# A constant product first, memory ahead of weights, deeper gate buffers, half of K later, two output products exchanged

## The chip, the cores and the metric

The kernel runs on one core of a Trainium2 chip. A core has a matrix engine (TensorE, PE in the profile; its weight loads are PEld), a vector engine (VectorE, DVE), a scalar engine (ScalarE, ACT), GpSimd (POOL) and SyncE (SP), each with an instruction line of its own that it works off in order, and 16 DMA engines that all queues share. SP, ACT and POOL issue the DMAs here. The metric is the device time of one execution in microseconds, lower is better; each time is the median of several runs.

## The reference

One block of a hybrid encoder on 512 frames of width 1024, all in float32:

```python
h = rms_norm(x, norm_mix_g)
proj = h @ w_in + b_in                       # 1024 -> 4864 columns
y_a = rwkv7_branch(proj[..., :1792], ...) @ w_branch_a
y_b = rglru_branch(proj[..., 1792:2304], proj[..., 2304:2816], ...) @ w_branch_b
merged = sigmoid(proj[..., 2816:3840]) * y_a + sigmoid(proj[..., 3840:]) * y_b
x = x + merged @ w_mix_out
x = x + cross_attention(rms_norm(x, norm_x_g), rms_norm(mem, norm_mem_g), w_cq, w_ckv, w_co)
x = x + conv_ffn(rms_norm(x, norm_ffn_g), w_ffn_in, ffn_conv_w, ffn_conv_b, w_ffn_out)
return rms_norm(x, norm_final_g)
```

Cross-attention has 4 heads of 256 channels over a memory of 256 rows; K and V are the two halves of `rms_norm(mem) @ w_ckv`. The conv FFN has 2816 hidden channels, a causal convolution of width 3 on the gate, and a GELU.

## The kernel before

Everything is kept with channels on the 128 partitions and the 512 frames along the free dimension; a "block" is 128 channels. A dense product is a sum over blocks of 128 input channels. For accuracy each operand is split into a high part in PE's fast float32 type and a low rest, and each 128 x 128 unit of weights gives three PE products (`mm3`, lines 161 to 163: high by high, high by low, low by high). Weights are streamed from DRAM in pieces of 512 KB, eight units each, through four raw buffers (`stream`, lines 96 to 117; `Units`, lines 132 to 149): SP issues the load, ACT casts the high part (line 115), DVE subtracts to get the low part (line 116); there are three buffers each for high and low.

The program text is not the order on the engines. A planner with a model of each instruction's duration sorts the instructions by a priority (the order of the text; `tc.high_priority` puts a block ahead) into a fixed line for each engine, before the kernel runs. `tc.keep_in_program_order`, `tc.issue_after` and `tc.add_manual_dep` fix the place of single instructions. A tile with `bufs=n` has n buffers in turn; a write into a buffer waits until the last reader of the tile n places before is done, and an instruction that waits holds up everything behind it in its engine's line.

The stages, in order:

- **Start (lines 269 to 303).** The memory (1 MB, tile `mraw`, four pieces of 256 KB, `load_m`) and the parameters `pv` are loaded. For K the memory is scaled with its norm's gain and split (lines 286 to 290, tile `m2`), its squares are summed (lines 291 to 294, `mss`) and turned into `rm`, the scale of each row of memory. SP's first loads are: memory piece 0, half of w_k's first piece, memory 1, the other half, memory 2, w_k's second piece, memory 3.
- **K and V (lines 306 to 348).** Eight blocks of K, 24 PE products of 256 columns each, written to DRAM through `kt`; then V, while x is loaded and normalised (`x_norm`, lines 323 to 330).
- **Small parameters (lines 354 to 397).** Constants of the two branches are worked out on DVE in the tile `dp`, from `pv`.
- **Projection and branches (lines 521 to 935).** 38 blocks of w_in (`inproj`), with the recurrences between them. The 16 gate blocks go to DRAM (`dG`). `NSUM` (line 517) says how many of POOL's DRAM-to-DRAM sums of FFN weights are released by each block (`sum_behind`): they prepare a Strassen-like scheme with seven products instead of eight for both FFN matrices.
- **Merge (lines 945 to 968).** For each of 8 blocks, w_branch_b's product (12 PE products of 512 columns) is multiplied with its gate `gb`, loaded back from `dG` by SP into two buffers (line 947); then the same for w_branch_a with `ga` (line 961, two buffers), whose result is added and split into `mg2`. The mix product (line 992) reads all of `mg2`.
- **Attention (lines 1018 to 1079).** K and V are loaded back by ACT's queue in four pieces (K's first half, V, V, K's second half) through two buffers `kv`, and split. Then for each head the scores, a softmax (`ex`, line 1057), the product with V, and in between the next head's q.
- **FFN in (lines 1141 to 1243)** and **FFN out (lines 1253 to 1374)**. FFN out is seven products over 4 x 11 units each, 132 PE products of 256 columns, named A11, A12, s1, s2, s3, s4, A22, in this order, with operands in three sets. `X` and `YZ` are their sums in PSUM. A product's weights named s come from DRAM (`dO`), where POOL has summed them; those of s4 are summed on top of those of s2 once these have been read (line 1366). Where a partial result is needed twice it is copied (`p1`, `p5`, `p6`). `ffn_out` adds a block to the residual `xr`, squares it and scales it with the final gain; `final` normalises a range of frames and stores it. The first half of the frames ends with A22 (`c21`, in two pieces of 128 frames, the last thing that is done), the second with s4 (`c12`).

Of the kernel before, what the change touches and what calls it, by code (L numbers as in the profile page):

```python
# [17 lines left out]
P = 128  # L18
T = 512
# [14 lines left out]
NMID = 10  # L34
IN_ORDER = IN_RWKV + IN_REST
# [19 lines left out]
def hybrid_block_kernel(ctx: ExitStack, tc: tile.TileContext, xT_d, mT_d, pv_d, cst_d, win_d, wk_d, wv_d,  # L55
# [213 lines left out]
    with tc.tile_pool(name="p0", bufs=1, reuse_waits="tile") as p0:  # L269
        ln_exp_set()  # L270
# [15 lines left out]
        for k in range(KB):  # L286
            g = par("nmem", k)
            S.activation(m2[:, 0, k, :], mraw[:, k, :], AF.Identity, scale=g)
            V.scalar_tensor_tensor(m2[:, 1, k, :], mraw[:, k, :], g, m2[:, 0, k, :].bitcast(F32),
                                   ALU.mult, ALU.subtract)  # L290
# [15 lines left out]
        for m in range(KB):  # L306
# [5 lines left out]
            kt = p0.tile([P, NMEM], F32, tag="kt", name=f"kt{m}", bufs=4)  # L312
            V.tensor_tensor(kt, ps[:, :NMEM], rm, ALU.mult)
# [40 lines left out]
        dp = cp.tile([P, 80], F32, name="dp")  # L354
        omu = dp[:, 0:14]
        V.tensor_scalar(omu, parall("mu"), -1.0, 1.0, ALU.mult, ALU.add)
        qb = dp[:, 14:28]
        V.tensor_tensor(qb, pv[:, PV["b_in"][0]:PV["b_in"][0] + 14], omu, ALU.mult)
        oka = dp[:, 28:32]
        V.tensor_scalar(oka, parall("k_a"), -1.0, 1.0, ALU.mult, ALU.add)  # L360

        cw = parall("cbw")
        bx = par("b_in", 14, 4)
        cbias = dp[:, 32:36]
        ccor = dp[:, 36:48].rearrange("p (j b) -> p j b", b=4)
# [1086 lines left out]
```

## Time and profile before

| | us |
|---|---|
| median of 3 runs | 908.43 (905.87 to 909.82) |
| the profiled execution, own time | 911.28 |
| its span | 909.5 |
| PE busy | 886.1 |
| DVE busy | 684.8 |
| ACT busy | 515.8 |

The span runs from the first instruction that the profiler saw to the last; 1.8 us of the execution's own time lie around it. "Busy" counts the time in which an engine has an instruction under way. In rows of the timeline the columns are start, duration, engine, line, operation, output <- inputs, shape, count, and in brackets the idle time before it with what ended it. PE's products overlap: a row lasts longer than the distance to the next one, and it is this distance that counts.

### The profile page before, as it was taken

Reading aid. Unit: us, or ns where it says so; the run is one execution under the profiler, and the core shown is the slowest. Engines: PE = TensorE matmul, PEld = TensorE weight load, DVE = VectorE, ACT = ScalarE, POOL = GpSimd, SP = SyncE. Lnnn points to the kernel's source line nnn. Section 1 sums busy time; section 2 is a strip of 40 time slices with the busy share of each in tenths; the row PEclk is TensorE's granted clock in tenths of the full one; section 3 lists DMA queues with packets and bytes.
Section 4 is the critical chain, followed back from the end, with each engine's and each line's share of the span. In section 5 each row is a group of like instructions: output and inputs, shape, how many; then the busy total and the mean of one; then the engine's idle time right before and its main releaser. Section 6 shows DMA issues by size and latency. Waiting matters only on the chain.

```text
span 909.5 us, 15907 instructions
## 1 busy us (share of the span) xinstructions
PE 886.1 (97%) x6186; PEld 769.3 (85%) x6186; DVE 684.8 (75%) x1100; ACT 515.8 (57%) x787; POOL 131.2 (14%) x161
## 2 busy tenths in 40 slices
PE   6999999999999999989989999999999999999996
PEld 6888878888877777768867778999999999999996
DVE  7884698768957686576566568889888888999674
ACT  6674676643347675134454356766655556757563
POOL 0102222021001122001012111111111111202100
PEclk9999999999999999999999999999999999999999
DMA  8879799677876289968887958899989998988963
GB/s 273 279 269 222 191 234 226 201 200 215 264 175 161 41 176 239 261 189 229 220 215 164 214 124 184 243 273 275 271 240 301 268 284 252 245 274 207 273 193 92
DMA packets 97642, 201.37 MB, mean 221 GB/s; under 512 B 19424, under 2 KB 30816, under 8 KB 97504
## 3 DMA queue, kind: packets, MB, share of 16 engines
q1 hardware_dynamic: 63584, 118.97, 40.0%
q0 software_dynamic: 25504, 67.38, 36.4%
q10 hardware_dynamic: 8480, 14.02, 4.5%
q8 instruction: 48, 0.79, 0.3%
q14 instruction: 26, 0.21, 0.1%
HBM read 188.54 MB, written 78.12 MB: 293 GB/s over the span
## 4 chain that ended last, share of the span: by engine, by line
PE 86%; DMA 7%; DVE 5%; ACT 1%; issue 1%; SPq 0%; DVEq 0%; ACTq 0%
PE in_ps L162 8%; PE in_ps L161 8%; PE in_ps L163 7%; PE fx_ps L162 5%; PE fx_ps L161 5%; PE fx_ps L163 5%; PE fyz_ps L162 3%; PE fyz_ps L163 3%; PE fyz_ps L161 3%; DMA gb<-dG 2%; PE ox_ps L163 2%; PE ox_ps L161 2%; PE ox_ps L162 2%; PE co_ps L161 2%; PE co_ps L163 2%; PE co_ps L162 2%
## 5 line engine op out<-in xcount | busy, mean ns | idle before, releaser
L127 ACT CAST wfi_h<-wfi_r 128x1024 fp32r<-128x1024 f32 x77 | 81.0, 1052 | 81.0 <-PE fyz_ps L162 28.4
L162 PE MATMUL in_ps<-hT,win_h 128*128 128x512 f32 x304 | 121.6, 402 | 0.0
L161 PE MATMUL in_ps<-hT,win_h 128*128 128x512 f32 x304 | 121.5, 401 | 0.1
L163 PE MATMUL in_ps<-hT,win_l 128*128 128x512 f32 x304 | 121.6, 401 | 0.0
L128 DVE TENSOR_TENSOR wfi_l<-wfi_r,wfi_h 128x1024 fp32r<-128x1024 f32 x77 | 94.1, 1222 | 23.0 <-ACT wfi_h L127 22.9
L427 POOL DMA_DIRECT2D dS<-in_wfi x66 | 66.5, 1028 | 267.8 <-PE in_ps L161 134.1
L116 DVE TENSOR_TENSOR win_l<-win_r,win_h 128x1024 fp32r<-128x1024 f32 x38 | 46.3, 1222 | 30.8 <-ACT win_h L115 30.1
L161 PEld LDWEIGHTS in_ps<-hT,win_h 128*128 128x128 f32 x304 | 57.0, 188 | 14.6 <-DVE pr L531 0.6
L162 PEld LDWEIGHTS in_ps<-hT,win_h 128*128 128x128 f32 x304 | 57.0, 188 | 14.5 <-issue 0.7
L163 PEld LDWEIGHTS in_ps<-hT,win_l 128*128 128x128 f32 x304 | 57.0, 188 | 14.2 <-issue 0.7
L463 POOL DMA_DIRECT2D dOs<-in_wfo x54 | 39.9, 789 | 188.4 <-PE fyz_ps L161 48.2
L115 ACT CAST win_h<-win_r 128x1024 fp32r<-128x1024 f32 x38 | 39.8, 1048 | 43.1 <-PE in_ps L162 40.4
L1279 DVE TENSOR_TENSOR wfo_l<-wfo_r,wfo_h 128x1024 fp32r<-128x1024 f32 (+1 forms) x39 | 47.1, 1209 | 16.2 <-ACT wfo_h L1278 14.6
L1278 ACT CAST wfo_h<-wfo_r 128x1024 fp32r<-128x1024 f32 (+1 forms) x39 | 40.4, 1038 | 30.2 <-DMA wfo_r<-dOs 8.0
L163 PE MATMUL ox_ps<-go,wfo_l 128*128 128x256 f32 x176 | 49.5, 281 | 1.2 <-DVE wfo_l L1279 1.2
L162 PE MATMUL fx_ps<-hr,wfi_h 128*128 128x256 f32 x176 | 49.8, 283 | 0.0
L161 PE MATMUL ox_ps<-go,wfo_h 128*128 128x256 f32 x176 | 49.8, 283 | 0.0
L163 PE MATMUL fx_ps<-hr,wfi_l 128*128 128x256 f32 x176 | 49.8, 283 | 0.0
L162 PE MATMUL fx_ps<-hq,wfi_h 128*128 128x256 f32 x176 | 49.4, 281 | 0.0
L162 PE MATMUL fyz_ps<-hq,wfi_h 128*128 128x256 f32 x176 | 49.4, 281 | 0.0
L161 PE MATMUL fx_ps<-hr,wfi_h 128*128 128x256 f32 x176 | 49.4, 280 | 0.0
L162 PE MATMUL ox_ps<-go,wfo_h 128*128 128x256 f32 x176 | 49.3, 280 | 0.0
(419 smaller groups left out, 2713.4 us busy)
## 6 DMA issues: line engine op xcount, KB each, us to landing
dS<-in_wfi POOLq DMA_DIRECT2D x66, 512.0 KB, 7.9
wfi_r<-dS SPq DMA_DIRECT2D x44, 512.0 KB, 6.3
win_r<-in_win SPq DMA_DIRECT2D x38, 512.0 KB, 5.6
wfi_r<-in_wfi SPq DMA_DIRECT2D x33, 512.0 KB, 5.9
dS<-dS POOLq DMA_DIRECT2D x22, 512.0 KB, 5.3
dOs<-in_wfo POOLq DMA_DIRECT2D x12, 512.0 KB, 7.1
wv_r<-in_wv SPq DMA_DIRECT2D x8, 512.0 KB, 4.9
dG<-gs ACTq DMA_DIRECT2D x16, 256.0 KB, 5.2
```

Source lines behind the costliest of these rows:

```text
L115: S.copy(hi[:, o:o + n], raw[:, o:o + n])
L116: V.tensor_tensor(lo[:, o:o + n], raw[:, o:o + n], hi[:, o:o + n].bitcast(F32), ALU.subtract)
L127: S.copy(hi, raw)
L128: V.tensor_tensor(lo, raw, hi.bitcast(F32), ALU.subtract)
L161: first = PE.matmul(ps, lh, rh, start=start, stop=False, **kw)
L162: PE.matmul(ps, lh, rl, start=False, stop=False, **kw)
L163: PE.matmul(ps, ll, rh, start=False, stop=stop, **kw)
L427: return lambda: nc.gpsimd.dma_start(s(out), src, **kw)
L463: yield lambda k=k, w=w, src=src: nc.gpsimd.dma_start(dO[n, m][:, k * P:(k + w) * P], src, **kw)
L1278: S.copy(hi[:, :n], raw[:, :n])
L1279: V.tensor_tensor(lo[:, :n], raw[:, :n], hi[:, :n].bitcast(F32), ALU.subtract)
```

## The change

The functions stay; the edits are these.

- **Start.** Ten PE products of a constant come first. The memory's gain is loaded by itself (`gm`, 8 columns) ahead of `pv`, which is issued later. SP's order becomes memory 0, half of w_k's piece, memory 1, the other half, memory 2, memory 3, w_k's second piece. The split of the memory is given high priority, the squares come after the last split, and `kt` has six buffers.
- **Small parameters.** The block is unchanged and comes behind the last evacuation of K.
- **NSUM.** Block 37 releases one sum, 17, 18 and 19 one more each, 20 two and 21 three fewer.
- **Merge.** `gb` takes turns over three tags with two buffers each, `ga` has five buffers.
- **Attention.** Three `kv` buffers; K's second half is loaded in the text after the first head.
- **FFN out.** A22 before s4. The copies `p6` go; the sum after s2 is added to `xr` at once. `c21` normalises the first half of the frames in one piece, `c12` the second in two pieces of 128.

```diff
+NWAKE = 10
+KVB = 3
...
-    wdma = []
+    wdma, mdma = [], []
...
                     elif len(wdma) == 1:
-                        tc.add_manual_dep(ins.ins, wdma[0].ins.name, mybir.DependencyInfo(
+                        tc.add_manual_dep(ins.ins, mdma[-1].ins.name, mybir.DependencyInfo(
...
+        wake = rw_ps("wake")
+        with tc.high_priority():
+            for i in range(NWAKE):
+                PE.matmul(wake, onesr, onesr.unsqueeze(1).to_broadcast([P, 4, P]), start=True, stop=True)
+        gm = cp.tile([P, KB], F32, name="gm")
+        o = PV["nmem"][0]
+        tc.keep_in_program_order(nc.scalar.dma_start(gm, pv_d[:, o:o + KB]))
         ln_exp_set()
...
-                tc.keep_in_program_order(
-                    nc.sync.dma_start(mraw[:, 2 * q:2 * q + 2, :], mT_d[:, 2 * q:2 * q + 2, :]))
-
-        nc.scalar.dma_start(pv, pv_d)
+                mdma.append(tc.keep_in_program_order(
+                    nc.sync.dma_start(mraw[:, 2 * q:2 * q + 2, :], mT_d[:, 2 * q:2 * q + 2, :])))
+
         load_m(0)
+        m2 = p0.tile([P, 2, KB, NMEM], F32R, name="m2")
+
+        def split_m(k):
+            g = gm[:, k:k + 1]
+            hi = S.activation(m2[:, 0, k, :], mraw[:, k, :], AF.Identity, scale=g)
+            V.scalar_tensor_tensor(m2[:, 1, k, :], mraw[:, k, :], g, m2[:, 0, k, :].bitcast(F32),
+                                   ALU.mult, ALU.subtract)
+            return hi
+
+        with tc.high_priority():
+            for k in range(2):
+                split_m(k)
         un = Units(wk_d, "wk")
         un.fill(lambda i: [load_m(q) for q in ((1,), (2, 3))[i]])
-        m2 = p0.tile([P, 2, KB, NMEM], F32R, name="m2")
+        tc.keep_in_program_order(nc.scalar.dma_start(pv, pv_d))
...
-        for k in range(KB):
-            g = par("nmem", k)
-            S.activation(m2[:, 0, k, :], mraw[:, k, :], AF.Identity, scale=g)
...
-        S.activation(mss, mraw[:, 0, :], AF.Square)
+        with tc.high_priority():
+            for k in range(2, KB):
+                last_m = split_m(k)
+        with tc.issue_after(last_m.ins):
+            S.activation(mss, mraw[:, 0, :], AF.Square)
         for k in range(1, KB):
-            S.activation(msq[k], mraw[:, k, :], AF.Square)
+            with tc.issue_after(last_m.ins):
+                S.activation(msq[k], mraw[:, k, :], AF.Square)
...
-            kt = p0.tile([P, NMEM], F32, tag="kt", name=f"kt{m}", bufs=4)
-            V.tensor_tensor(kt, ps[:, :NMEM], rm, ALU.mult)
+            kt = p0.tile([P, NMEM], F32, tag="kt", name=f"kt{m}", bufs=6)
+            last_k = V.tensor_tensor(kt, ps[:, :NMEM], rm, ALU.mult)
...
-        dp = cp.tile([P, 80], F32, name="dp")
+        with tc.issue_after(last_k.ins):
+            dp = cp.tile([P, 80], F32, name="dp")
...
-            17: 3, 18: 4, 19: 4, 20: 4, 21: 4}
+            37: 1, 17: 4, 18: 5, 19: 5, 20: 2, 21: 1}
...
-        gb = tp.tile([P, T], F32, tag="st", name=f"gb{m}", bufs=2)
+        gb = tp.tile([P, T], F32, tag=("ga", "gx", "st")[m % 3], name=f"gb{m}", bufs=2)
...
-        ga = pm.tile([P, T], F32, tag="ga", name=f"gta{m}")
+        ga = pm.tile([P, T], F32, tag="ga", name=f"gta{m}", bufs=5)
...
-    for i, what in ((0, "K"), (0, "V"), (1, "V"), (1, "K")):
-        kv = pk.tile([P, D], F32, tag="kv", name=f"kv{what}{i}", bufs=2)
+
+    def load_kv(what, i):
+        kv = pk.tile([P, D], F32, tag="kv", name=f"kv{what}{i}", bufs=KVB)
...
+    load_kv("K", 0)
+    for i in range(2):
+        load_kv("V", i)
...
         if hd < 3:
             q2 = q_head(hd + 1)
+        if hd == 0:
+            load_kv("K", 1)
...
-        for n in ("A11", "A12", "s1", "s2", "s3", "s4", "A22"):
+        for n in ("A11", "A12", "s1", "s2", "s3", "A22", "s4"):
...
+    def c21(m):
+        sq = ffn_out(X[m], None, ALU.subtract, MQ + m, cols[0], last=m == MQ - 1)
+        if m == MQ - 1:
+            final(cols[0], sq, 2, "x")
+
     def c12(m):
-        sq = ffn_out(YZ[m][:, H:T], p6[m], ALU.add, m, cols[1], last=m == MQ - 1)
-        if m == MQ - 1:
-            final(cols[1], sq, 2)
...
         if m < MQ - 1:
-            ffn_out(X[m], None, ALU.subtract, MQ + m, cols[0])
+            ffn_out(YZ[m][:, H:T], None, ALU.add, m, cols[1])
         else:
-            for o in (0, P):
+            for o in (H, H + P):
                 ts = slice(o, o + P)
-                final(ts, ffn_out(X[m][:, ts], None, ALU.subtract, MQ + m, ts, last=True), 4)
+                final(ts, ffn_out(YZ[m][:, ts], None, ALU.add, m, ts, last=True), 4, "yz")
...
-    out_product("s2", 0, X, False, lambda m: S.copy(p6[m], X[m]))
+    out_product("s2", 0, X, False,
+                lambda m: V.tensor_tensor(xr[:, m, cols[1]], xr[:, m, cols[1]], X[m], ALU.add))
...
+    out_product("A22", 0, X, False, c21)
     out_product("s4", 1, [t[:, H:T] for t in YZ], False, c12)
-    out_product("A22", 0, X, False, c21)
```

More of the change, by code (lines that the diff above doesn't have):

```diff
@@ L351, in hybrid_block_kernel @@
             nc.sync.dma_start(cst, cst_d)
-        dp = cp.tile([P, 80], F32, name="dp")
[L355 to L365, printed above, removed]
@@ L1308, in hybrid_block_kernel @@
     sn1, sn5 = ([pc.tile([P, T], F32, tag="sn", name=f"{n}_{i}", bufs=3) for i in range(2)] for n in ("o1", "o5"))
-    sn6 = pc.tile([P, T], F32, tag="sn", name="o6_0", bufs=3)
     p1, p5 = ([t[:, c] for t in ts for c in cols] for ts in (sn1, sn5))
-    p6 = [sn6[:, c] for c in cols]
-    p6 += [pc.tile([P, H], F32, tag="p5", name=f"o6_{m}", bufs=3) for m in (2, 3)]
     def ffn_out(src, snap, sign, m, ts, first=False, last=False):
@@ L1327, in ffn_out, with final @@
         return sq
-    def final(ts, sq, nb):
+    def final(ts, sq, nb, tag):
         n = ts.stop - ts.start
-        pss = rw_ps(f"rs_ps{ts.start}", pf, "yz", bufs=4)
+        pss = rw_ps(f"rs_ps{ts.start}", pf, tag, bufs=4)
         PE.matmul(pss[:, :n], ones, sso[:, ts], start=True, stop=False)
```

75 lines of the change are left out of this document (41 added, 34 removed).

## The prediction

> **What bounds the kernel now.** I read the page first, then the view of waits for PE (TensorE), because the page says that this engine is the bound.
>
> ```profile
> span 909.5 us, 15907 instructions
> PE 886.1 (97%) x6186; PEld 769.3 (85%) x6186; DVE 684.8 (75%) x1100; ACT 515.8 (57%) x787; POOL 131.2 (14%) x161
> ```
>
> PE is idle for 909.5 - 886.1 = 23.4 us. Nothing in the change removes a needed product, so it can only win from these idle times and from products that run slowly. The view of waits (wait, total us, times, longest) says where they are:
>
> ```profile
> PE k_ps L161 <- ACT m L288: 6.5, 1, 6.5
> PE sc_ps L1050 <- ACT ex L1057: 2.6, 1, 2.6
> PE mix_ps L161 <- ACT mg L967: 1.3, 1, 1.3
> PE ya_ps L161 <- DVE mB L951: 1.3, 2, 0.7
> PE ox_ps L163 <- DVE wfo_l L1279: 1.2, 2, 0.8
> PE mix_ps L162 <- DVE mg L968: 0.7, 1, 0.7
> PE ya_ps L161 <- DVE gta L965: 0.3, 1, 0.3
> ```
>
> Four places: the start (6.5), the merge of the gated branches (ya and mix, 3.6 in five waits), attention (2.6) and the output weights (1.2). They sum to 13.9 us; the other 9.5 I put down to the tail after the last product, which no edit shortens. Each edit aims at one of the four, so I price them in turn, always as later or earlier starts of PE's products.
>
> **1. The start.** The timeline of the first 16 us, and one stretch of the windows (us, then busy time and count for PE, PEld, DVE, ACT, POOL, then clock, DMA share, GB/s):
>
> ```profile
> 1.05 0.23 DVE L198 CAST onesr<-ones 128x128 fp32r<-128x128 f32 x1
> 5.41 0.62 ACT L115 CAST wk_h<-wk_r 128x512 fp32r<-128x512 f32 x1 [0.48 <-DMA wk_r<-in_wk]
> 6.49 0.58 PE L161 MATMUL k_ps<-m,wk_h 128*128 128x256 f32 x1 [6.49 <-ACT m L288]
> 8.22 0.41 PE L163 MATMUL k_ps<-m,wk_l 128*128 128x256 f32 x1
> 8.43 0.41 PE L161 MATMUL k_ps<-m,wk_h 128*128 128x256 f32 x1
> 9.06 0.91 ACT L288 ACTIVATE m<-mraw,pv 128x256 fp32r<-128x256 f32 x2 [0.91 <-DMA mraw<-in_mT]
> 11.55 1.23 DVE L116 TENSOR_TENSOR wk_l<-wk_r,wk_h 128x1024 fp32r<-128x1024 f32 x1
> 12.83 0.39 PE L163 MATMUL k_ps<-m,wk_l 128*128 128x256 f32 x1 [0.47 <-DVE wk_l L116]
> 15.16 0.28 PE L162 MATMUL k_ps<-m,wk_h 128*128 128x256 f32 x1
> 15.27 0.28 PE L163 MATMUL k_ps<-m,wk_l 128*128 128x256 f32 x1
> 6.50:13.00 6.50, 5.91 (x22) 4.89 (x23) 5.83 (x17) 5.59 (x14) 0.00 (x0) 1.00 0.94 361
> ```
>
> At 8 us products start 0.21 us apart, at 15 us 0.115 apart: PE starts at half rate, although the clock column says 1.00. Until 13.0 it does 22 products, which at full rate would be 22 x 0.115 = 2.5 us of work. The ten wake products need only onesr (ready at 1.28). A product of 512 columns at half rate takes about 2 x 0.21 = 0.42 us, so they run from 1.3 to 5.5, before anything real can begin; they cost nothing on PE and no other engine waits for them.
>
> But data sets this stretch as well. The first product can move from 6.49 to the end of the first w_k cast, 5.41 + 0.62 = 6.03, since the first casts of m, for which PE now waits, come ahead of the squares and need the small gm instead of the whole pv. Then four blocks of m give 12 products; the next need the third piece of memory, which landed at 9.06, and its casts (0.45 on ACT, as long on DVE): not before 9.9. With this landing the earliest time for 22 products is 9.9 + 10 x 0.115 = 11.1, a gain of 13.0 - 11.1 = 1.9, and 2.5 if the memory, now whole ahead of w_k's second piece, lands 0.6 sooner. The second piece however lands later, behind 256 KB more, and its casts come after the four of m: ACT is at 9.06 + 4 x 0.45 = 10.9 free for it, and 1.03 and 1.23 us later (the row at 11.55) its low half is there: 13.1. By then PE has done the first piece's 24 products and perhaps 3 more, 5 more than before: 5 x 0.115 = 0.6. I take **-0.8**, near this end because it is the chain that the static order gives, with bounds of -2.5 and +1.5 (the squares later, so that PE's sum over mss stands in its line before mss is ready).
>
> A rule of the Trainium skill (TensorE: Matmul & The Clock Gate, Part 1) bears on the ten products: the gate opens after a busy window of about 3.4 us that runs free of the kernel, so a start may meet it anywhere in its window. By that rule the wake's 4.2 us may or may not hold a whole busy window, and the gate opens between 4.7 and 8.1, an estimate from that page. The trace's 6.49 to somewhere past 8.43 fits it. It changes little here, because the products up to 9.9 wait for data in either case.
>
> The block of small parameters (lines 354 to 397) moves behind the last K evacuation:
>
> ```profile
> L389 DVE TENSOR_TENSOR dp<-dp x7: 155/159/164, 18.2 to 40.9; 128x4 f32<-128x4 f32 x7
> ...
> 36.00:57.00 21.00, 20.98 (x91) 16.50 (x90) 18.55 (x31) 16.77 (x22) 1.08 (x2) 1.00 0.89 302
> ...
> 49.41 1.42 DVE L328 SCALAR_TENSOR_TENSOR hf<-xraw,pv,rx 128x512 f32<-128x512 f32 x2 [0.45 <-ACT rx L214]
> ```
>
> It is 37 DVE instructions of about 0.16 us, 5.9 us (the first row gives the duration and the stretch of seven of them). Until now they filled gaps from the start on; after, they come in the stretch 36 to 57 or later, where DVE is idle 21.00 - 18.55 = 2.45 us and some of them run already. From 49.4 its line is full with the normalised x, for which the first product of w_in waits. What doesn't fit has lower priority than x's chain and can slip behind it, since the scans need only its first two results. I count 0, with +6 as the far end (all of it ahead of x). The deeper kt buffers count 0: no PE wait names kt.
>
> **2. The merge.** DVE waits in the stretch 340 to 410, the DMA view of 345 to 410, and four rows of the timeline:
>
> ```profile
> DVE mB L951 <- DMA gb<-dG: 9.8, 6, 3.0
> DVE gta L965 <- DMA gta<-dG: 3.0, 5, 1.0
> ...
> gb<-dG SPq DMA_DIRECT2D x8, 256.0 KB, 6.7
> gta<-dG SPq DMA_DIRECT2D x8, 256.0 KB, 3.3
> ...
> 344.93 0.50 SPq L948 DMA_DIRECT2D gb<-dG  x1
> 350.52 9.52 SPq L948 DMA_DIRECT2D gb<-dG  x3
> ...
> 373.73 0.40 PE L163 MATMUL yb_ps<-yb,wbb_l 128*128 128x512 f32 x1
> 374.81 0.47 PE L161 MATMUL ya_ps<-ya,wba_h 128*128 128x512 f32 x1 [0.68 <-DVE mB L951]
> ```
>
> With two buffers a gate's load is issued only when the product two blocks back is evacuated, and lands 6.7 us later, while a block lasts 12 x 0.233 = 2.8 us. So the gates are always late, banks of PSUM stay full and PE waits. The last two rows show how a wait is sized: starts are 1.08 apart instead of 0.23, so 0.85 is lost where the view says 0.68. Five waits therefore cost 3.6 + 5 x 0.17 = 4.4 us.
>
> After: gb has six buffers. The yb blocks ended every 2.8 us up to 374.0, the first at 354.4; the seventh load needs the first's buffer, is issued at about 355, lands at 362 and is wanted at 371. All eight are early. gta has five: the sixth needs the first block's buffer, free about 8 us after ya begins, and lands 3.3 to 6.7 later, at 11 to 15; it is wanted at 6 x 2.8 = 17. The eighth's margin is about the same, and the mix reaches the last mg only 21 x 0.233 = 4.9 us after ya's end, against a chain of four 0.7 us steps. So 4.4 could all go. The loads share SP's queue in order with w_ba's and w_mix's pieces, and a load that waits for its buffer holds those up; I leave 0.6 for that: **-3.8**, bounds -4.5 and 0. NSUM takes five POOL sums from the two blocks before the merge and gives four of them to earlier ones; 0, as no PE wait names them.
>
> **3. Attention.** Rows from the timelines of ACT, DVE and PE:
>
> ```profile
> 456.24 1.23 DVE L1029 TENSOR_TENSOR K<-kvK,K 128x1024 fp32r<-128x1024 f32 x1 [1.30 <-ACT K L1028]
> ...
> 458.81 0.38 ACTq L1024 DMA_DIRECT2D kvK<-dK  x1
> ...
> 466.42 1.05 ACT L1028 CAST K<-kvK 128x1024 fp32r<-128x1024 f32 x1 [3.90 <-DMA kvK<-dK]
> ...
> 468.00 0.39 PE L161 MATMUL q_ps<-hx,wq_h 128*128 128x512 f32 x1
> 470.30 0.56 ACT L1057 ACTIVATE ex<-sc_ps,smst,rxc 128x256 f32<-128x256 f32 x1 [1.40 <-DVE smst L1055]
> 471.01 0.39 PE L1050 MATMUL sc_ps<-K,q 128*128 128x256 f32 x1 [2.62 <-ACT ex L1057]
> ```
>
> K's second half is loaded at 458.81, lands 7.6 us later, and ACT stands 3.90 us before its cast, with the first softmax queued behind. PE's starts are 471.01 - 468.00 = 3.01 apart: 2.8 lost. Heads 0 and 1 don't need this half. After, K0, V0, V1 have their own buffers and load at once, and K1's cast comes after the first head. I take **-2.4**, since the first softmax still shares DVE with w_q's low halves. The end on the other side: K1's cast stands in ACT's line elsewhere.
>
> **4. The output.** A row of the chain, and two of the timeline:
>
> ```profile
> 832.75 11.11 DMA wfo_r<-dOs
> ...
> 828.24 1.64 POOL L463 DMA_DIRECT2D dOs<-in_wfo  x2 [25.68 <-DMA wfo_r<-dOs]
> 843.95 2.20 ACT L1278 CAST wfo_h<-wfo_r 128x1024 fp32r<-128x1024 f32 x2 [4.45 <-DMA wfo_r<-dOs]
> ```
>
> The two waits there (1.2 + 2 x 0.17 = 1.5) are for weights of s2 and s3 that load while POOL's sums for s4 run. Those sums are released by s2's loads as before, so swapping s4 and A22 behind s3 leaves both waits. Four ACT copies become four DVE adds and four later adds go: hidden behind PE. The tail after the last product has the same steps with the halves of the columns exchanged. **0**, bounds -1.5 and +1.0.
>
> **Sum.** -0.8 - 3.8 - 2.4 + 0 = -7.0. The profiled execution has a span of 909.5 and took 911.28 by its own time, so it would be 904.3; it is 2.85 above the median of the runs, 908.43, and there the same step gives **901.4 us**.
>
> **Rivals.**
> - The start gains nothing: squares or parameter block meet PE or x's chain. For it: DVE has no gap from 49.4 on. Against: the planner gives both a lower priority. Term 1 becomes +1.5: 903.7.
> - The merge keeps its waits: SP's queue holds a gate behind a weight or a weight behind a gate. For: one queue, 9.52 us for three issues. Against: the margins above. Term 2 becomes -0.6: 904.6.
> - The change doesn't do what it says in attention: K0's buffer falls free at 457.5, so K1 is loaded nearly when it is now and the planner puts its cast in the same place. Term 3 becomes -0.4: 903.4.
> - Slower: K1's cast stands in ACT's line in front of the second head's softmax, before its load has landed. Of the present stand of 3.90 PE lost 2.8, so 1.1 is covered. The longest landing on the chain of waits is 11.1 us; standing for all of it costs 10.0, against the 2.4 won, so term 3 becomes +7.6: 911.4. The kernel is slower than before from a stand of 1.1 + 7.0 = 8.1 us on. For it: ACT's line is fixed in advance and its present stand shows a landing later than planned. Against: after the second head's products there is more than a head's time until K1 is wanted.
> - PE falls back to half rate between 5.5 and 9.9, where it has 1.4 us of work. Then products until about 13 start 0.21 apart, as now, and term 1 is about +0.5: 902.7. No row here shows a fall back. The Trainium skill (TensorE: Matmul & The Clock Gate, Part 1) has the gate close after an idle window of about 3.4 us, which would be this case.
>
> **How the numbers follow.** Forecast 0.52, more than it (899.5 and below, most bounds met) 0.10, start 0.12, merge 0.10, K in its old place 0.09, slower 0.04, half rate 0.03. About 0.5% (4.5 us) is what a measurement of this kernel can tell from no change. Below 903.9 lie forecast, more, half rate, K and half of the start case: 0.80. The slow case at 911.4 is above 912.9 only with a part of another loss: 0.03. Within 0.5%: 0.17. Low end: all bounds of gain, 908.4 - 2.5 - 4.5 - 2.8 - 1.5 = 897.1, taken as 897.0. High end: two of the losing cases together, 901.4 + 2.3 + 3.2 = 906.9, taken as 906.5.
>
> **What would show it.** Right: products 0.115 apart from the first k_ps on; DVE no longer waits for gb or gta in the waits, and the ya and mix rows are gone from PE's; no wait of sc_ps over 1 us; both ox_ps waits still there. Wrong: a wait of rs_ps or in_ps before 70 us, ACT standing for kvK after the first head, or new waits of PE in stretches that the change doesn't touch, from a different static order.

## The result, and the profile after

| | before | after |
|---|---|---|
| median of 5 runs | 908.43 (905.87 to 916.71) | 898.08 (897.30 to 899.19) |
| profiled execution, own time | 911.28 | 897.30 |
| its span | 909.5 | 895.5 |

The ratio is 0.9878, with a 95% interval of 0.9844 to 0.9912: 10.35 us faster by the medians, where 7.0 were forecast. The profiled execution of before lay 2.85 us above its median and that of after 0.8 below, so the two traces differ by 14.0.

The page and the view of PE's waits of the kernel after (wait, total us, times, longest) stand against the rows shown of before:

```profile
PE 882.4 (99%) x6196; PEld 772.1 (86%) x6196; DVE 685.8 (77%) x1100; ACT 514.6 (57%) x783; POOL 131.3 (15%) x161
...
PE wake L276 <- DVE Pp L583: 1.3, 1, 1.3
PE k_ps L165 <- DVE wk_l L118: 0.8, 1, 0.8
PE in_ps L163 <- ACT hT L350: 0.6, 1, 0.6
PE k_ps L163 <- ACT wk_h L117: 0.4, 1, 0.4
PE yb_ps L164 <- DVE yb L966: 0.4, 1, 0.4
```

The rows of ya_ps, mix_ps, sc_ps and ox_ps are gone, and idle time falls from 23.4 to 895.5 - 882.4 = 13.1 us. But 10 us of idle time less don't make 14 us of span, and the ten products of a constant count as busy now:

```profile
1.33 4.63 PE L276 MATMUL wake<-onesr 128*128 128x512 f32 x10 [1.33 <-DVE Pp L583]
```

They fill 4.5 us, up to the first product of K at 5.81. Without them PE has 10.3 - 4.5 = 5.8 us less idle time, and the other 8.2 of the 14.0 us must be needed products that follow each other more closely. Setting the first PE products of the stages of both timelines against each other shows where the time went. Each column is the time from one stage's first product to the next one's (for the first, from the span's start; for the last, to the last product; the tail behind it, 8.3 us in both, is left out):

| stage | before | after | difference | forecast |
|---|---|---|---|---|
| start to the first in_ps | 57.61 | 56.81 | -0.80 | -0.8 |
| first in_ps to first psw | 44.80 | 45.72 | +0.92 | 0 |
| psw to first ga | 156.41 | 154.67 | -1.74 | 0 |
| ga to first yb_ps | 90.96 | 90.88 | -0.08 | 0 |
| yb_ps to first q_ps (merge and mix) | 96.28 | 89.19 | -7.09 | -3.8 |
| q_ps to first co_ps (attention) | 70.53 | 66.85 | -3.68 | -2.4 |
| co_ps to first fx_ps | 51.35 | 51.34 | 0.0 | 0 |
| fx_ps to first ox_ps (FFN in) | 220.22 | 220.35 | +0.1 | 0 |
| ox_ps to last product (FFN out) | 113.00 | 111.38 | -1.62 | 0 |

Two things in it were in no term. First, psw to ga got shorter, a stretch that no edit touches. In the timeline of PE the first and the last of the 192 mix products after show why; below them are the 28th, behind the last wait, and the last of before:

```profile
393.32 0.39 PE L163 MATMUL mix_ps<-mg,wmix_h 128*128 128x512 f32 x1
...
437.05 0.39 PE L165 MATMUL mix_ps<-mg,wmix_l 128*128 128x512 f32 x1
```

```profile
407.56 0.39 PE L163 MATMUL mix_ps<-mg,wmix_l 128*128 128x512 f32 x1
...
445.83 0.39 PE L163 MATMUL mix_ps<-mg,wmix_l 128*128 128x512 f32 x1
```

(437.05 - 393.32) / 191 = 0.2290 us from start to start. Before, (445.83 - 407.56) / 164 = 0.2333, and the neighbours of in_ps, yb_ps and ya_ps that met no wait stood as far apart. Nothing in the change touches a product. What did change is the place of the operands: the new tile gm takes 32 bytes per partition, and every later buffer in SBUF stands 32 bytes higher.

Second, what the start won is given back by psw. In the timelines of DVE and PE after:

```profile
49.59 0.16 DVE L419 TENSOR_SCALAR dp<-dp 128x4 f32<-128x4 f32 x1
49.66 1.22 DVE L118 TENSOR_TENSOR wv_l<-wv_r,wv_h 128x1024 fp32r<-128x1024 f32 x1
50.80 1.41 DVE L349 SCALAR_TENSOR_TENSOR hf<-xraw,pv,rx 128x512 f32<-128x512 f32 x2
...
60.71 0.73 PE L163 MATMUL in_ps<-hT,win_h 128*128 128x512 f32 x2 [0.59 <-ACT hT L350]
```

The last instruction of the block of small parameters now starts at 49.59, and the normalised x starts behind it at 50.80 instead of 49.41. PE waits for hT at 60.71, which it did not before.

### The profile page after: what moved, and what is told of

The parts are those of the page before. It is cut to its first block, busy times and chain, and to the rows that moved or that the text cites. A ratio compares the mean times of both kernels' runs of the same rounds, so it can differ in the third digit from the quotient of the medians.

```text
span 895.5 us, 15930 instructions
## 1 busy us (share of the span) xinstructions
PE 882.4 (99%) x6196; PEld 772.1 (86%) x6196; DVE 685.8 (77%) x1100; ACT 514.6 (57%) x783; POOL 131.3 (15%) x161
## 4 chain that ended last, share of the span: by engine, by line
PE 93%; DVE 4%; ACT 1%; issue 1%; DMA 1%; SPq 0%; DVEq 0%; ACTq 0%
PE in_ps L164 7%; PE in_ps L165 7%; PE in_ps L163 7%; PE fx_ps L163 5%; PE fx_ps L164 5%; PE fx_ps L165 5%; PE fyz_ps L164 4%; PE fyz_ps L163 3%; PE fyz_ps L165 3%; PE ox_ps L164 2%; PE ox_ps L163 2%; PE ox_ps L165 2%; PE oyz_ps L164 2%; PE oyz_ps L163 2%; PE oyz_ps L165 2%; PE co_ps L163 2%
## 5 line engine op out<-in xcount | busy, mean ns | idle before, releaser
L130 DVE TENSOR_TENSOR wfi_l<-wfi_r,wfi_h 128x1024 fp32r<-128x1024 f32 x77 | 93.9, 1219 | 23.4 <-ACT wfi_h L129 23.1
L449 POOL DMA_DIRECT2D dS<-in_wfi x66 | 66.6, 1028 | 293.0 <-PE in_ps L163 111.6
L485 POOL DMA_DIRECT2D dOs<-in_wfo x54 | 39.9, 784 | 180.3 <-PE fx_ps L163 44.5
L163 PE MATMUL fx_ps<-hq,wfi_h 128*128 128x256 f32 x176 | 49.3, 280 | 0.0
L164 PE MATMUL fx_ps<-hq,wfi_h 128*128 128x256 f32 x176 | 49.3, 280 | 0.0
```

The lines of the kernel that those rows point to most:

```text
L130: V.tensor_tensor(lo, raw, hi.bitcast(F32), ALU.subtract)
L163: first = PE.matmul(ps, lh, rh, start=start, stop=False, **kw)
L164: PE.matmul(ps, lh, rl, start=False, stop=False, **kw)
L449: return lambda: nc.gpsimd.dma_start(s(out), src, **kw)
L485: yield lambda k=k, w=w, src=src: nc.gpsimd.dma_start(dO[n, m][:, k * P:(k + w) * P], src, **kw)
```

## The experiments

Twelve kernels were run, each against the kernel before on the same chip. The table gives their medians and, from the profile of each, the stages that matter (us, as above; "all edits" is the changed kernel run again).

| run | median, kernel before beside it | to in_ps | in_ps to psw | psw to ga | merge, mix | attention | co_ps to fx_ps | FFN out |
|---|---|---|---|---|---|---|---|---|
| e1: before, 32 bytes higher | 906.30, 909.33 | 59.3 | 44.0 | 154.7 | 94.9 | 67.4 | 51.2 | 112.7 |
| e2: after, 96 bytes higher | 903.91, 909.33 | 59.3 | 46.0 | 156.9 | 91.2 | 68.7 | 51.4 | 111.2 |
| e3: small parameters free | 900.51, 909.33 | 60.8 | 44.7 | 154.7 | 89.2 | 66.9 | 51.2 | 111.7 |
| e4: old gate buffers | 899.44, 909.33 | 59.8 | 44.5 | 154.7 | 89.7 | 68.9 | 51.2 | 111.4 |
| e5: all edits | 896.54, 908.95 | 56.4 | 44.5 | 154.6 | 89.2 | 67.0 | 51.2 | 111.4 |
| e6: old table of sums | 898.88, 908.95 | 56.6 | 44.6 | 154.7 | 90.4 | 67.0 | 51.2 | 111.4 |
| e7: old buffers, old table | 906.29, 908.95 | 58.9 | 44.2 | 154.7 | 96.3 | 67.1 | 51.2 | 111.4 |
| e8: old loads of K and V | 897.56, 908.95 | 56.8 | 44.5 | 154.7 | 89.2 | 67.3 | 51.2 | 111.4 |
| e9: no wake products | 898.71, 910.22 | 57.6 | 45.7 | 154.7 | 89.2 | 66.8 | 51.2 | 111.4 |
| e10: old output order | 897.48, 910.22 | 56.6 | 45.2 | 154.7 | 89.2 | 66.9 | 51.2 | 111.7 |
| e11: o2 moved, block earlier | 898.63, 910.22 | 59.9 | 44.3 | 154.7 | 89.2 | 66.9 | 51.3 | 111.7 |
| e12: weights moved too | 900.61, 910.22 | 57.7 | 45.1 | 156.3 | 90.5 | 67.3 | 50.4 | 111.6 |

The changed kernel run again (e5) was expected at 897 to 900 us and took 896.54. Its stages agree with those of its first profile within 0.4 us but for in_ps to psw, which is 1.2 shorter: PE did not wait for hT there. That wait stands in four of the nine profiles in which the block of small parameters is placed as in the change (after, e2, e9, e10; not e4 to e8). One profile stands for each run, so a stage of the table carries the chance of one execution.

**e1 and e2: the place of the operands.** One puts the shift into the kernel before, the other takes it out of the changed one.

```diff
+        gm = cp.tile([P, KB], F32, name="gm")      # e1, in the kernel before
+        nc.gpsimd.memset(gm, 0.0)
...
-        gm = cp.tile([P, KB], F32, name="gm")      # e2, in the changed kernel
+        gmt = cp.tile([P, 32], F32, name="gm")
+        gm = gmt[:, 0:KB]
```

> The kernel before, with one unused tile of 32 bytes per partition ahead of the small parameters, so that every later buffer in SBUF stands 32 bytes higher, as in the changed kernel. No instruction of the kernel moves. In the trace of before, products of 512 columns with hT, yb, ya and mg as the moving operand start 0.233 us apart, in the trace after 0.229, and these buffers went from 32 to 64 bytes above a multiple of 128. Theory A (the place of the moving operand sets the spacing): 0.229 here in in_ps, yb_ps, ya_ps and mix_ps, still 0.233 in v_ps and co_ps, and about 1300 x 0.0042 = 5.4 us less time than before. Theory B (the spacing differs from execution to execution, or comes from the changed order): 0.233 everywhere and no change in time.

> The changed kernel with its small tile gm made 128 bytes wide instead of 32, so that every later buffer has the same place in its multiple of 128 bytes as in the kernel before; the order of the work is that of the changed kernel. Theory A: the spacing goes back to 0.233 in in_ps, yb_ps, ya_ps and mix_ps, and the time is about 5 us more than the changed kernel's, 903, which is 5 to 6 us below before and what the order of the work alone brought. Theory B: 0.229 stays and the time is the changed kernel's 898.

In the timelines of PE, first the 28th and the last mix product of e1, which stand closer than those of before; then the first and the last of e2, the same in number and order as after, which are slow again:

```profile
405.90 0.39 PE L163 MATMUL mix_ps<-mg,wmix_l 128*128 128x512 f32 x1
...
443.45 0.39 PE L163 MATMUL mix_ps<-mg,wmix_l 128*128 128x512 f32 x1
```

```profile
399.49 0.39 PE L163 MATMUL mix_ps<-mg,wmix_h 128*128 128x512 f32 x1
...
444.23 0.40 PE L165 MATMUL mix_ps<-mg,wmix_l 128*128 128x512 f32 x1
```

(443.45 - 405.90) / 164 = 0.2290 in e1, (444.23 - 399.49) / 191 = 0.2342 in e2. In e1 in_ps, yb_ps, ya_ps and mix_ps stand 0.229 apart, in e2 0.234; v_ps keeps 0.233 in both and co_ps 0.2325 and 0.2331. So the place sets the spacing: shown in both directions. The size is less sure. The ratio of e1 is 0.9957 (0.9930 to 0.9983): 3.0 us by the medians, 1.5 to 6.4 by the interval, where 5.4 were expected. By the stages the faster products pay where PE is the bound: psw to ga, with 573 of them, gained 1.7 in e1 and lost 2.2 in e2, the merge and mix gained 1.4 (with other waits than before, see e7) and lost 2.0, but ga to yb, where 147 of them stand between the recurrences' small products, moved by 0.2. e2's ratio of 0.9938 (0.9915 to 0.9962) is about what the order of the work alone brings, 5.4 us by the medians; as the products of e2 stand 0.0009 further apart than those of before, it could be up to 1296 x 0.0009 = 1.2 us more.

**e3: the block of small parameters.**

```diff
-        with tc.issue_after(last_k.ins):
+        if True:
             dp = cp.tile([P, 80], F32, name="dp")
```

> The changed kernel without the rule that holds the block of small parameters behind the last K evacuation; everything else stays. Theory: in the changed kernel the block stands in VectorE's line at 44.3 to 49.7 ahead of the normalised x (whose rx was ready at 48.6), and PE then waits 1.4 us in the first in_ps products. Freed, the block fills gaps from about 16 us on again, the first hf starts near 48.6 instead of 50.8, the in_ps waits between 59 and 63 us go, and the first psw product starts up to 1.4 us earlier than 102.5: the time falls by 0.5 to 1.4 us. Rival: the stretch from 66 to 135 us is bound by VectorE's own chain, so what the start wins is given back there and the time stays (within 0.3 us); or the block in the gaps holds back w_k's low halves and PE loses at 10 to 30 us what it wins at 60.

DVE and PE in e3's timeline:

```profile
12.68 0.17 DVE L378 TENSOR_SCALAR dp<-pv 128x14 f32<-128x14 f32 x1 [2.64 <-DMA pv<-in_pv]
...
14.02 1.22 DVE L118 TENSOR_TENSOR wk_l<-wk_r,wk_h 128x1024 fp32r<-128x1024 f32 x1
...
15.29 0.39 PE L165 MATMUL k_ps<-m,wk_l 128*128 128x256 f32 x1 [3.77 <-DVE wk_l L118]
15.52 0.33 PE L163 MATMUL k_ps<-m,wk_h 128*128 128x256 f32 x1
...
16.08 0.41 PE L163 MATMUL k_ps<-m,wk_h 128*128 128x256 f32 x1
16.29 0.41 PE L164 MATMUL k_ps<-m,wk_h 128*128 128x256 f32 x1
```

The rival. The first instruction of the block needs pv, which the change issues late; freed, it stands 2.64 us at the head of DVE's line with w_k's low half behind it, and PE starts its next product at 15.29, 2.85 us later than in e5 (12.44), and then runs at half rate, 0.21 us from product to product. The in_ps wait is gone, as expected, though e5 has none either, and 4.4 us are lost up to in_ps against e5. The edge to K's last evacuation belongs to the late load of pv, and my forecast counted it at 0 without seeing what it protects.

**e4, e6, e7: the merge.** Buffers undone, table undone, both undone.

```diff
-        gb = tp.tile([P, T], F32, tag=("ga", "gx", "st")[m % 3], name=f"gb{m}", bufs=2)   # e4, e7
+        gb = tp.tile([P, T], F32, tag="st", name=f"gb{m}", bufs=2)
...
-        ga = pm.tile([P, T], F32, tag="ga", name=f"gta{m}", bufs=5)
+        ga = pm.tile([P, T], F32, tag="ga", name=f"gta{m}")
...
-            37: 1, 17: 4, 18: 5, 19: 5, 20: 2, 21: 1}                                     # e6, e7
+            17: 3, 18: 4, 19: 4, 20: 4, 21: 4}
```

> The changed kernel with the gates' buffers of the merge as before: two for gb under the tag st, two for ga. The small tile gm stays, so the places of hT, yb, ya and mg stay too. By the forecast the waits of ya_ps and mix_ps come back and the stretch from the first yb_ps to the first q_ps gets 3.8 to 4.4 us longer (89.2 in the changed kernel, 96.3 before): 93.0 to 93.6. If the buffers had brought all of the 7.1 us that this stretch lost, it is 96.3 again. If they had brought nothing, 89.2.

> The changed kernel with the table of POOL's weight sums as before: five more of them in the two blocks ahead of the merge, fewer in earlier blocks. The gates keep their new buffers. My forecast gave the table 0 and the buffers 3.8. Theory A (the buffers do it): the stretch from the first yb_ps to the first q_ps stays at 89.2 us and no ya_ps or mix_ps wait comes back. Theory B (the sums' traffic delays the gates, and with the table undone it does so again, buffers or not): 90 to 93. The undone buffers alone cost this stretch 0.5 us, which speaks against A having all 3.8.

> The changed kernel with both the gates' buffers and the table of sums as before; the places in SBUF stay new. If buffers and table each suffice to clear the merge (each alone undone costs little), both undone bring the waits back: yb to q 92.5 to 95, as in the shifted kernel before (94.9), and 3 to 5 us more time than the changed kernel. If neither matters and the waits in the two profiles of the old order came by chance from late landings, 89 to 90.

DVE's waits for the gates, first in e4, then in e7; PE in e7's timeline, and a view of e7 by stretches (from:to, length, busy time and count of PE, PEld, DVE, ACT, POOL, then the granted clock, DMA share, GB/s):

```profile
DVE mB L973 <- DMA gb<-dG: 4.4, 4, 2.0
DVE gta L987 <- DMA gta<-dG: 1.1, 1, 1.1
```

```profile
DVE mB L973 <- DMA gb<-dG: 10.1, 5, 5.3
DVE gta L987 <- DMA gta<-dG: 1.0, 1, 1.0
```

```profile
368.79 0.40 PE L165 MATMUL yb_ps<-yb,wbb_l 128*128 128x512 f32 x1
372.88 0.80 PE L163 MATMUL yb_ps<-yb,wbb_h 128*128 128x512 f32 x1 [3.69 <-DVE mB L973]
373.48 0.63 PE L164 MATMUL yb_ps<-yb,wbb_h 128*128 128x512 f32 x1
373.90 0.63 PE L165 MATMUL yb_ps<-yb,wbb_l 128*128 128x512 f32 x1
...
378.60 0.46 PE L164 MATMUL ya_ps<-ya,wba_h 128*128 128x512 f32 x1
378.90 0.40 PE L165 MATMUL ya_ps<-ya,wba_l 128*128 128x512 f32 x1
```

```profile
364.00:369.00 5.00, 5.00 (x23) 3.93 (x21) 2.43 (x3) 1.05 (x1) 0.00 (x0) 1.00 1.07 240
369.00:373.00 4.00, 0.31 (x2) 0.12 (x1) 0.69 (x1) 0.00 (x0) 0.00 (x0) 0.86 0.89 305
373.00:378.60 5.60, 5.60 (x14) 4.36 (x15) 2.71 (x4) 0.57 (x1) 0.00 (x0) 0.50 0.63 183
378.60:384.00 5.40, 5.40 (x25) 4.44 (x24) 3.60 (x5) 1.13 (x3) 0.00 (x0) 0.99 0.94 302
```

The buffers alone undone cost the stretch 89.7 - 89.2 = 0.5 us, the table alone 1.2, both 7.1. So either edit nearly clears the merge. For e4 this is next to "brought nothing" of its expectation. e6 lies between its two theories: at the low end of B, with mix_ps waits of 0.4 and 0.2 us, but most of the 7.1 is won by the buffers alone, as A has it. For e7 it is more than the 92.5 to 95 and the 3 to 5 us that were expected. The five sums that the old table puts into the two blocks ahead of the merge share the DMA engines with the gates' loads, and the median gb lands 7.1 us after its issue in e7, 5.1 in e4: with two buffers and the new table (e4) DVE still waits 4.4 us for gb, but no wait of PE comes of it that the view lists; with two buffers and the old table (e7) it waits 10.1. e7's median is 9.75 us above e5's; in the profiles, 10.6 apart, the merge has 7.1 of it, the start 2.4 and FFN in 1.2.

The rows of e7 also show how one wait costs more than its length: 3.69 us of waiting, then 14 products 0.43 us apart at a granted clock of 0.50. (The 0.86 in the row of the wait is 1.1 us at half, so the clock fell before the wait was over.) Of the 4.1 us from 368.79 to 372.88 3.9 are lost, and 14 x 0.2 = 2.8 behind it: 6.7 together. e1, with the old merge, shows the same wait (3.43 us) and the same fall at the same place; the profile of before has five shorter ones in its stead and keeps its clock. The Trainium skill (TensorE: Matmul & The Clock Gate, Part 1) has the clock halve after an idle window of about 3.4 us. The waits of 3.43, 3.69 and 3.77 us in e1, e7 and e3 agree with it.

But the clock also falls in the start of e2, e4, e7 and e11, without such a wait. The same view of e2, e4 and e7, in each a stretch ahead of the fall and the one behind it:

```profile
6.49:9.90 3.41, 1.87 (x11) 1.42 (x10) 1.58 (x3) 1.65 (x4) 0.00 (x0) 1.00 0.94 348
9.90:16.70 6.80, 6.12 (x25) 5.59 (x26) 5.74 (x11) 6.51 (x14) 0.00 (x0) 0.50 0.72 257
```

```profile
7.90:11.30 3.40, 1.67 (x11) 1.27 (x10) 1.98 (x5) 1.89 (x5) 0.00 (x0) 1.00 1.02 404
11.30:18.10 6.80, 6.34 (x28) 5.76 (x27) 5.72 (x9) 5.11 (x10) 0.00 (x0) 0.50 0.65 221
```

```profile
10.10:13.50 3.40, 2.12 (x14) 1.62 (x13) 2.75 (x5) 3.40 (x7) 0.00 (x0) 1.00 0.85 339
13.50:16.90 3.40, 3.40 (x17) 3.40 (x18) 3.30 (x6) 2.28 (x5) 0.00 (x0) 0.50 0.61 186
```

In e11 the clock is at 0.50 from 11.7 to 18.5. The longest single wait in these starts is 1.7 us (e2, for m), 1.6 (e4), 0.8 (e7) and 2.0 (e11), and PE was busy for 1.67 to 2.12 us of the 3.4 ahead of the fall. e12, busy for 2.17 of 3.4 (8.1 to 11.5), keeps its clock; where the limit lies is not shown. Part of the long starts in the table is late data: the second piece's low half is there at 14.24, 13.97, 13.34 and 13.88 in e2, e4, e7 and e11, against 12.44 in e5. The other part, 1.1, 1.9, 1.5 and 2.1 us, is lost behind it at half rate.

**e8: K's second half.**

```diff
-KVB = 3
+KVB = 2
...
-    load_kv("K", 0)
-    for i in range(2):
-        load_kv("V", i)
+    for i, what in ((0, "K"), (0, "V"), (1, "V"), (1, "K")):
+        load_kv(what, i)
...
-        if hd == 0:
-            load_kv("K", 1)
```

> The changed kernel with attention's loads as before: two buffers, K's second half loaded and cast before the first head. Forecast: the wait of the first sc_ps comes back and q to co is 2.4 to 2.8 us longer than 66.85, so 69.3 to 69.7. Rival: the shifted kernel before had the old loads, no sc_ps wait and 67.4, so the wait depends on when the half lands; then 67.0 to 67.5, and the edit is worth about 0.5 us in such an execution. New waits of prT_ps for the softmax (1.16 us in two variants of the new order) would be gone here.

Attention takes 67.3 us against 67.0 in e5, with no wait of sc_ps and none of prT_ps: the rival. In ACT's timeline, first after (the first head's softmaxes and K's second half), then e8:

```profile
454.65 0.57 ACT L1083 ACTIVATE ex<-sc_ps,smst,rxc 128x256 f32<-128x256 f32 x1 [2.44 <-DVE smst L1081]
...
455.20 0.56 ACT L1083 ACTIVATE ex<-sc_ps,smst,rxc 128x256 f32<-128x256 f32 x1
...
457.15 1.04 ACT L1051 CAST K<-kvK 128x1024 fp32r<-128x1024 f32 x1
458.09 0.56 ACT L1083 ACTIVATE ex<-sc_ps,smst,rxc 128x256 f32<-128x256 f32 x1
```

```profile
448.36 0.38 ACTq L1047 DMA_DIRECT2D kvK<-dK  x1
...
453.11 1.05 ACT L1051 CAST K<-kvK 128x1024 fp32r<-128x1024 f32 x1 [0.84 <-DMA kvK<-dK]
```

With the old loads the half lands 453.11 - 448.36 = 4.75 us after its issue and ACT stands 0.84; in the profile of before it took 7.6 and ACT stood 3.90. That execution had a late landing, and the wait of sc_ps is a matter of chance, not of every execution. The edit moves the cast back by two of the first head's four softmaxes, not behind the head. So it has its own price when the half is late: in e4 ACT stands 1.73 us before it, PE then waits 1.2 us for prT_ps, and attention takes 68.9 (e2 has the same wait and 68.7). In the other nine profiles of the new loads it takes 66.9 to 67.3, with the old ones 67.3 (e8), 67.4 (e1) and 70.5 (before): where no landing is late, no gain can be told from the scatter.

**e9: the wake products.** The loop runs 0 times instead of 10.

> The changed kernel without the ten products of a constant; nothing else moves. Forecast's theory: products up to about 13 us start 0.21 to 0.4 us apart instead of 0.12 from the first or third one on, but the pieces of w_k and memory set the end of this stretch in either case (last waits wk_l, near 12.5), so the time changes by less than 0.5 us. Rival: the slow products push the first piece's 24 products past the second piece's casts and the stretch up to the first v_ps gets 1.5 to 2.5 us longer than 33.6.

In e9's timeline the K products start 0.21 apart until about 11.3 and the second piece's low half is waited for at 13.17; in e5 they are at 0.12 from 6.9 on, with that wait at 12.44. Up to the first v_ps it is 34.2 against 33.56, up to in_ps 57.6 against 56.4, between the two expectations. But ACT's timeline, e9 first and then e5, shows a landing that differs:

```profile
9.40 0.91 ACT L294 ACTIVATE m<-mraw,gm 128x256 fp32r<-128x256 f32 x2 [0.86 <-DMA mraw<-in_mT]
```

```profile
7.87 1.71 ACT L294 ACTIVATE m<-mraw,gm 128x256 fp32r<-128x256 f32 x4 [0.62 <-DMA mraw<-in_mT]
```

In e9 the last quarter of the memory lands later and ACT stands 0.86 us for it, ahead of the second piece's casts. The 13.17 - 12.44 = 0.73 us are this chain's, and by the end of K the delay is no larger; the other 0.4 up to in_ps arise far behind, in V's stage. So the slow products cost nothing that the rows show up to there, as the forecast's theory has it, and a gain of the ten products is not shown. e9 does not fall back to half rate behind 11.3; of the ten profiles with these products and the same start (after, e2, e4 to e8, e10 to e12) four do.

**e10: the output's order.** The edits to `out_weights`, `final`, `c12`, `c21` and the copies `p6` undone.

```diff
-        for n in ("A11", "A12", "s1", "s2", "s3", "A22", "s4"):
+        for n in ("A11", "A12", "s1", "s2", "s3", "s4", "A22"):
...
-    out_product("A22", 0, X, False, c21)
     out_product("s4", 1, [t[:, H:T] for t in YZ], False, c12)
+    out_product("A22", 0, X, False, c21)
```

> The changed kernel with the output product's order as before (s4 ahead of A22, the four copies of s2 by ScalarE). My forecast gave the new order 0 because it left both waits of ox_ps; the stretch from the first ox_ps to the last product is 111.4 us in all runs of the new order, 113.0 and 112.7 in the two of the old. Theory: 112.7 to 113.0 again, with one or two waits of ox_ps for wfo_l of 0.4 to 0.8 us, and 1.4 us more time. Rival: the old order's waits come from elsewhere (POOL's table, the stretch's later start in time) and it stays at 111.4.

The rival again: 111.7 with the old order, and no wait of ox_ps for wfo_l. That is 0.3 us more than e5, but e3 and e11 have the new order and 111.7 too (e3 with a wait of 0.3 for wfo_l), so the order alone has no price that can be told here. The waits of 0.4 to 0.8 us stand only in before and e1, which have the old order and the old table of sums; e6 and e7 have the old table with the new order and 111.4. Whether either edit suffices or the two waits hung on landings of those two executions stays open, with one profile each.

**e11 and e12: which place is the good one.**

```diff
-    rxc = pb.tile([P, 4], F32, name="rxc")
+    rxc = pb.tile([P, 20], F32, name="rxc")[:, 0:4]                      # e11 and e12: o2 64 bytes up
...
-            last_k = V.tensor_tensor(kt, ps[:, :NMEM], rm, ALU.mult)
+            done_k = V.tensor_tensor(kt, ps[:, :NMEM], rm, ALU.mult)     # e11 and e12
+            last_k = done_k if m <= NDP else last_k                      # NDP = 3
...
+    wpad = ctx.enter_context(tc.tile_pool(name="wpad", bufs=1)).tile([P, 16], F32, name="wpad")   # e12
+    nc.gpsimd.memset(wpad, 0.0)
     wp = ctx.enter_context(tc.tile_pool(name="wp", bufs=3))
...
-        gm = cp.tile([P, KB], F32, name="gm")                               # e12
+        gmt = cp.tile([P, 24], F32, name="gm")
+        gm = gmt[:, 0:KB]
```

> The changed kernel with two edits: the block of small parameters waits for the fourth K evacuation instead of the last, and rxc's tile is 64 bytes wider, so that o2 stands 64 bytes above a multiple of 128 (it stood at 0, and at 96 in the kernel before), and so do q2 and ex behind it. Theory A (moving operand at 64): co_ps goes from 0.2325 to 0.229 us, so 192 x 0.0035 = 0.7 us less between the first co_ps and the first fx_ps (51.2 to 50.5). Theory B (something else makes the merge's products fast): co_ps stays. The block: no in_ps wait for hT near 60 us, in to psw 44.5 or less; if instead it gets in the way of w_k's low halves, a wk_l wait of over 1 us between 20 and 35.

> The previous kernel with the pool of weight tiles moved up by 64 bytes and the places of all the others kept in their multiples of 128, so that now the weights too stand at 64. V's products are the only ones of 512 columns whose moving operand is a weight (wv). Theory A1 (only the moving operand's place counts): v_ps goes from 0.233 to 0.229, in_ps and the others stay at 0.229, 0.4 us less. Theory A2 (what counts is that moving and stationary operand differ by 64): in_ps, yb, ya and mix go back to 0.233 and the time is about 5 us more, v_ps (moving 64, stationary m at 64) stays at 0.233.

The first and last co_ps products, in e11 and in e12:

```profile
505.77 0.40 PE L164 MATMUL co_ps<-o,wo_h 128*128 128x512 f32 x1
...
556.86 0.39 PE L166 MATMUL co_ps<-o,wo_l 128*128 128x512 f32 x1
```

```profile
507.72 0.39 PE L166 MATMUL co_ps<-o,wo_h 128*128 128x512 f32 x1
...
557.88 0.39 PE L168 MATMUL co_ps<-o,wo_l 128*128 128x512 f32 x1
```

Neither of my rules holds. With o2 64 bytes above a multiple of 128 co_ps did not get faster (51.09 us from first to last, neighbours without a wait 0.2334 apart), but with the weights moved too it did (50.16, and 0.2274). in_ps, yb_ps, ya_ps and mix_ps went back to 0.2325 in e12, as A2 has it (with 2.0 us more than e11 by the medians where 5 were expected), and v_ps only to 0.2322. After the fact, one rule fits the moving operand of five of the seven groups of products: fast at 192 bytes above a multiple of 256. By the program's allocation hT, yb, ya and mg stand there after and in e1 (160 before, 32 in e2, 64 in e12), and o2 stands there only in e12 (224 before, 0 after, 96 in e2, 64 in e11). v_ps, whose wv stands there in e12, gains a quarter of what it should, and q_ps, whose operand stands there after, half (0.2308). This was not tried by itself: what is shown is that the place matters, by up to 2%, and not which rule it follows.

The block of small parameters held back to the fourth K evacuation gave 44.3 from in_ps to psw in e11 and no in_ps wait; but e7, with the block behind the last one, has 44.2 and none either, so no gain of it is shown. No run was clearly faster than the changed kernel: e5, e10 and e11 at 896.5 to 898.6 are not told apart.

## Why the prediction came out as it did

The forecast of 901.4 us was 3.3 too high, with its direction and range right; 898.1 lies in the case "more than it", which had a chance of 0.10. That it lies inside the range at all is in part luck. The order of the work alone brought about 5.4 us (e2; 3.5 to 7.7 by the interval of the ratio) where 7.0 were forecast, and the places of the operands, which no term had, the rest (3.0 by themselves in e1, 1.5 to 6.4 by the interval). In the pair of profiles merge, attention and output each went beyond their bounds of gain (-4.5, -2.8, -1.5), as the profiled execution of before lay 2.85 us above its median. Of the four terms the start's number came out, the merge was mis-sized with a wrong step in it, and attention and output were read from waits that not every execution has:

- **Start, -0.8.** -0.8 and -1.2 up to in_ps in the two profiles of the changed kernel. The mechanism of the sum held: the second piece's low half, priced at 13.1, was there at 12.6 and 12.4, and by 12.0 the trace after has 26 products of K, against 22 by 13.0 before. The size is luck: over the ten profiles with this start the stretch takes 56.4 to 59.9, with the old one 57.6 (before) and 59.3 (e1). The long ones have late memory (PE waited 1.6 to 2.0 us for m in e2, e4 and e11) and a fall of the clock, so the term's upper bound of +1.5 was too low for a single execution. The ten products "cost nothing", rightly, and no gain of theirs is shown (e9). The parameter block at 0 is 0 in one of the two profiles and takes 1.2 in the other, where it meets x's chain: the first rival, for a part of its price.
- **Merge, -3.8.** -7.1 in the profile, of which 384 x 0.0043 = 1.65 is spacing and 5.4 waits. The step that failed is "NSUM 0, as no PE wait names them": the sums name themselves in no wait because they act through the landing of the gates, and the new table alone brings 6.6 of the 7.1 us between e7 and e5 (e4). The buffers, on which the term was built, bring 5.9 alone (e6), so their mechanism held and was priced too low. The term was also sized by one execution's five short waits; e1 and e7 show one long wait and a halved clock in their place, 5.7 to 7.1.
- **Attention, -2.4.** The step that failed is the wait of 2.8 us taken from one trace as if every execution had it. With the old loads e1 and e8 have none, and the edit is worth at most 0.3 there (e8). The third rival described what the planner did, for the most part: the cast moved by two softmaxes.
- **Output, 0.** -1.6. The step "swapping s4 and A22 leaves both waits" is wrong as a forecast of the profile: both went. But the old order alone doesn't bring them back (e10), so the swap is not shown to have removed them, and the 0 that the edit was given stands. What did remove them stays open.
- **Half rate.** The rival said that no row shows a fall back. Later rows do: e1 and e7 in the merge, e2, e3, e4, e7 and e11 in the start. In the four starts with the change's own order (all but e3) it cost 1.1 to 2.1 us, where the rival was given 1.3, and it came in four of ten profiles, where its chance was 0.03. In the changed kernel's own two profiles the products are at full rate from 6.9 on.
- **The signs named for "right".** Products 0.115 apart from the first k_ps: from the fourth on. No DVE wait for gb or gta, no ya and mix rows, no sc_ps wait: as said. Both ox_ps waits still there: wrong. Of the signs named for "wrong" one came, a wait of in_ps (0.6 us at 60.71) and of rs_ps (0.3 at 18.6) before 70 us.

## What to carry to other kernels

A wait seen in one profile is a sample: before a term is built on it, ask whether it hangs on a landing, and look at the scatter of the runs (902.9 to 914.6 over 23 runs of before, 897.3 to 899.2 over the 5 of after). The same start took 56.4 to 59.9 us in ten profiles, so a difference of 1 us between two single profiles shows nothing by itself. When two edits aim at the same wait, undo each alone and both together; here each looked nearly worthless alone, and both together 7 us. And compare early the distance between neighbouring products: a tile of 32 bytes that nobody reads moved it by 2% (e1).

## What the runs showed of the hardware

- The distance between products of 512 columns depends on where the operands lie in SBUF: 0.2290 (after) and 0.2342 (e2) for the same 192 products in the same order, 0.2334 and 0.2274 at best for co_ps (e11, e12). Which rule it follows stays open.
- In a wait of 3.69 us the granted clock fell from 1.00 to 0.50 and stayed there for 5.7 us behind it, so that the wait cost nearly twice its length (e7). The clock also fell without any wait longer than 2.0 us, where PE was busy for 1.67 to 2.12 us of the 3.4 ahead (e2, e4, e7, e11), and then stayed at 0.50 for 3.4 us (e7) or 6.8 (the others).
- The same load of K's second half took 4.75 us in one execution (e8) and 7.6 in another (before).
